# Last modulation beside w_o, seven products from the second FFN slab on, and another order of pairs in the last projection

## The chip, the cores and the metric

The kernel runs on one core of a Trainium2 chip. The metric is the device time of one execution in microseconds; the time before is the median of three runs. All times in the text are microseconds.

## The reference

One layer of a decoder trunk on x of 256 rows (SEQ) by 2048 columns (D), with a condition c; all in f32.

```python
# each layer
mod = SiLU(c) @ ada_w + ada_b -> (shift1, scale1, gate1, shift2, scale2, gate2)
h   = RMSNorm(x) * (1 + scale1) + shift1
h @ w_in + b_in  -> RG-LRU input, GeLU gate, q, k, v, branch gates
branch A: conv -> RG-LRU * GeLU(gate) -> w_lru
branch B: sliding-window attention -> w_att
merged = sigmoid(g_A) * A + sigmoid(g_B) * B
x  += gate1 * (merged @ w_o)
h2  = RMSNorm(x) * (1 + scale2) + shift2
x  += gate2 * SwiGLU(h2)          # hidden width 5632
out = RMSNorm(x)
```

## The kernel before

**Products.** Every f32 weight block is split into a high part `hi` (f32r, cast by ACT, L305) and a rest `lo` (`raw - hi`, DVE, L317), and so is every activation. A product is then three matmuls in `mm3`: L355 (hi by hi), L356 (lo of one side), L357 (lo of the other). A matmul has 512 columns in all the places that matter here.

**Items.** The program is a list of items, each one load of 512 KB (128 x 1024 f32, `raw`, L288, on SP's queue) and twelve matmuls as a rule. `step(i)` emits one item after the other: it issues the load of item i + 5, makes hi up to item i + 3 and lo up to item i + 2, then the matmuls. `raw` has five buffers, `hi` four, `lo` three. Since each engine and each DMA queue works in the order of emission, this sets what stands behind what. SP's queue holds nearly all DMAs.

**Work on the side.** Beside the items, generators (`Side`) emit attention, scan and modulations in small steps. A planner (`run_sides`) emits a step when its own estimate of the busy times of PE, DVE, ACT and DMA has room before the end of the present item, and when the condition that the step yields is true. It charges 1.46 per load of 512 KB, and nothing for the loads of xr, g1 and x1d.

**Modulations.** The first five are made by `ada_cols` (L496: multiply and reduce, 158 halves `aw` of 512 KB). The sixth, gate2, is made by `ada_rows` (the side `ada_ffn`): 32 loads `aw` of 512 KB (L467), a memset of `pa` on POOL (L677), a load of the bias row into `pa` (L678, SP), 32 DVE rows that accumulate `aw * c` into `pa` (L685), and four small products with a row of ones that spread the sum over the partitions (L691, L693). It starts when the condition of its first `yield` is true. The buffer of `pa` is shared with the row of c that `ada_cols` uses.

**Stages, by item number of before.** 244 to 275: w_o, four slabs of eight items. At its start `w_o_first` loads x again as `xr0` to `xr3` (L1034) and sends gate1 through memory: `g1_row` is copied by ACT (L1013), written as `g1d` (L1015) and read back broadcast as `g10`, `g11` (L1018). Each w_o slab ends with `yo = wo * g1` (L1055; L1100 in the last) and `xr += yo` (L1057, L1101), and the result is kept in `x1d` (L1041). After w_o comes the second norm (L1100 to L1141), and then eleven FFN slabs: `fg` and `fu`, whose result `ft` is transposed by PE (L954). Slabs below `SLAB_7` are plain (`add_slab`, 192 matmuls). From `SLAB_7` on `add_pair` computes three of the eight 2 x 2 quads of blocks (k = 4, 8, 12) by Winograd's form with seven products instead of eight (`seven`), whose sums of weights, `made`, are emitted by DVE (L418 to L425) into buffers that `ada_rows` uses as well; `all_modulations` therefore finishes `ada_ffn` ahead of slab `SLAB_7`.

**Last projection.** It has two sweeps over pairs k = 0, 2, 4, ... of hidden blocks: n = 0 (`w_f2a`) and n = 2 (`w_f2d`). The pairs in `SEVEN` (6, 10, ..., 34) are Winograd quads (`seven_last`: sums `last`, `ah`, `al`), the others plain. The pairs from `EARLY` (36) on are plain and, in the second sweep, follow as items of other matrices. After the last quad `combined(n)` (L1390 to L1399) adds the shared products, and `blocks` (L1415, L1417, L1441) adds the residual and norm weight to finished blocks. The blocks of the first sweep are finished beside the start of the second one. The program ends with the late products, the last norm (L1469 to L1515) and the stores.

Of the kernel before, what the change touches and what calls it, by code (L numbers as in the profile page):

```python
# [21 lines left out]
NH = HID // P  # L22
# [40 lines left out]
N_MADE, N_HOLD = 5, 4  # L63
SEVEN = tuple(range(6, 36, 4))

SEVEN_1, SLAB_7 = (4, 8, 12), 3
EARLY = NH - 2 * N_HOLD

N_SPARE = 5
# [5 lines left out]
def hybrid_layer(  # L75
# [19 lines left out]
    def free(b4=0, m=0):  # L95
        used["b4"] -= b4
        used["m"] -= m
# [11 lines left out]
    def mtile(name):  # L109
        used["m"] += 1  # L110
        return sum_bank(name)
# [372 lines left out]
    def ada_cols(todo, halves):  # L484

        yield 0, 0
        for group in todo:
            for j in range(2):
                for m, kt in group:
                    v = V_ADA + m * NK + kt  # L490
                    dst = modc[:, m, kt:kt + 1]
                    if not halves.got:
                        halves.fetch()
                    yield CH * T_DVE + 0.1, 0, 0, 0, halves.here
                    r = halves.take()
                    nc.vector.tensor_tensor_reduce(  # L496
                        out=r, in0=r, in1=crow[:, j * CH:(j + 1) * CH], op0=ALU.mult, op1=ALU.add, scale=1.0,
                        scalar=dst if j else vec[:, v:v + 1], accum_out=dst,
                    )
                    halves.fetch()  # L500
            for m, kt in group:
                if m in (1, 4):
                    g, dst = (V_N1 if m == 1 else V_N2) + kt, modc[:, m, kt:kt + 1]
                    nc.vector.scalar_tensor_tensor(dst, dst, 1.0, vec[:, g:g + 1], op0=ALU.add, op1=ALU.mult)
                cols_done.add((m, kt))
# [162 lines left out]
    def ada_rows():  # L668

        got = Halves([ada_g[kt, :, j * CH:(j + 1) * CH] for kt in range(NK) for j in range(2)])  # L670
        got.spare = lambda: len(got.got) - got.own < N_SPARE
        yield 0, 0, 0, 0, lambda: bool(h2)
        streams.append(got)
        got.fetch()

        pa = ap_.tile([P, D], F32, tag="pal", name="pa")
        nc.gpsimd.memset(pa, 0.0)  # L677
        nc.sync.dma_start(pa[0:1, :], bg_row)  # L678
        for kt in range(NK):
            for j in range(2):  # L680
                if not got.got:
                    got.fetch()
                yield CH * T_DVE, 0, 0, 0, got.here
                p = pa[:, j * CH:(j + 1) * CH]
                nc.vector.scalar_tensor_tensor(p, got.take(), cact[:, kt:kt + 1], p, op0=ALU.mult, op1=ALU.add)  # L685
                got.fetch()
        for c in range(4):
            yield 0, 0, 0, 1
            pb = mtile(f"pb{c}")
            cs = slice(c * 512, (c + 1) * 512)  # L690
            nc.tensor.matmul(pb, lhsT=ones, rhs=pa[:, cs], start=True, stop=True)  # L691
            yield 0, 0.55
            nc.scalar.copy(pa[:, cs], pb)  # L693
            free(m=1)
        bcs[5] = pa
# [393 lines left out]
    h2, h_sum = {}, {}  # L1089
# [241 lines left out]
    def out_products(jobs, t2=(0, 1), hold=None, after=None):  # L1331

        def go(hi, lo):
            if hold is not None:
                hold.extend((hi, lo, j) for j in jobs)
            if jobs[0][:2] == (0, 0):
                last_first()
                sides.append(Side(fetch_last()))
            for t in t2:
                for kt in sorted({j[0] for j in jobs}):  # L1340
                    ah, al = fact(kt)
                    mine = [j for j in jobs if j[0] == kt]
                    for k, (l, w) in enumerate(((ah, hi), (ah, lo), (al, hi))):
                        for _, n, c0 in mine:
                            nc.tensor.matmul(  # L1345
                                bank(t, n), lhsT=l[:, rows(t)], rhs=w[:, c0:c0 + 512], start=kt == 0 and k == 0,
                                stop=kt == (EARLY - 2 if (t, n) == (1, 3) else NH) - 1 and k == 2, skip_group_check=True,
                            )
            if after is not None:
                after()  # L1350
        return go

    def seven_last(k, n, src):
        parts = {}

        def parts_high():
            hi = parts[0] = wp.tile([P, 8, P], F32R, tag="araw", name=f"ah{n}_{k}", bufs=N_ADA)
            nc.scalar.copy(hi[:, 0:7, :], f_sum[k][:, 0:7, :])
            return 0, 0.9

        def parts_low():
            lo = parts[1] = b4(f"al{n}_{k}", F32R, (8, P))
            nc.vector.tensor_tensor(lo[:, 0:7, :], f_sum[k][:, 0:7, :], f32(parts[0][:, 0:7, :]), op=ALU.subtract)
            return 1.0, 0

        def own(to):
            if to not in "pqru":
                return bank(int(to[0]), n + int(to[1]))
            if k == SEVEN[0]:
                fin[to] = sum_bank(f"p{to}{n}")  # L1370
            return fin[to]

        items[-3].before.append(parts_high)
        items[-2].before.append(parts_low)
        seven(
            (src[k], src[k + 1]), {(0, 0): (0, 0), (0, 1): (0, 512), (1, 0): (1, 0), (1, 1): (1, 512)},
            lambda a: [parts[h][:, a, :] for h in range(2)], own, k == SEVEN[0], k == SEVEN[-1],
            lambda i: fin["made"][:, i * CH:(i + 1) * CH], (lambda: combined(n)) if k == SEVEN[-1] else None,
        )
# [46 lines left out]
    def blocks(n0, n1):  # L1426

        def post():
            last = None
            for n in range(n0, n1):  # L1430
                for t in range(2):
                    g = residual(t, n)
                    next(g)
                    if last is not None:
                        next(last, None)
                    last = g
                    yield 1.2, 0.7
            next(last, None)
            for t in range(2):
                x2 = fin["x2"][:, t, n0 * 512:n1 * 512]  # L1440
                nc.vector.tensor_tensor(x2, x2, fin["fg"][:, n0 * 512:n1 * 512], op=ALU.mult)  # L1441
                yield 0.6 * (n1 - n0), 0.7 * (1 - t)
        return post

    for n, src in ((0, w_f2a), (2, w_f2d)):
        for k in range(0, NH if n == 0 else EARLY, 2):
            if k in SEVEN:
                seven_last(k, n, src)
                continue
            for kt in (k, k + 1):  # L1450
                items.append(Item(
                    src[kt], CH, out_products([(kt, n, 0), (kt, n + 1, 512)]), blocks(0, 2) if kt == NH - 1 else None,
                ))
# [74 lines left out]
    todo = iter([(decay, 0)] + [(f, g) for f in (lru, attention) for g in range(4)])  # L1528
    mix = [Side(mixers(todo)) for _ in range(2)]
    ada_ffn = Side(ada_rows())  # L1530

    cols = [[(m, kt) for m in (1, 0) if m == 0 or kt >= N_K] for kt in range(NK)]
# [4 lines left out]
    ada = Side(ada_cols(cols, halves), 3)  # L1537
# [151 lines left out]
```

## Time and profile before

| what | us |
|---|---|
| median of three runs | 1553.1 |
| range of the three | 1551.76 to 1557.28 |
| the profiled execution, its own time | 1555.14 |
| its span in the trace | 1553.4 |
| PE busy | 1534.8 (99%) |
| DVE busy | 1359.0 (87%) |
| ACT busy | 843.8 (54%) |
| mean granted clock of PE | 0.997 |
| w_o on PE | 743.4 to 831.9 |
| the 32 rows of `pa` (L685) | 860.8 to 955.1 |

PE is the matmul engine, PEld its weight load, which overlaps it. DVE makes all `lo` parts and adds, ACT the `hi` parts, POOL does almost nothing, and SP issues the DMAs. In a timeline a row has start, duration, engine, line, operation, output and inputs, the number of instructions drawn together, and in brackets the idle time before and what ended it. A matmul's duration there (0.39) is that of a pipelined instruction; the distance of two starts is what it costs. The rows of the windows view give stretch and length, then the busy time of PE, weight load, DVE, ACT and POOL with numbers of instructions, the granted clock, the share of the DMA engines and GB/s.

### The profile page before, as it was taken

How to read it: one execution, taken by the hardware profiler on the slowest of the kernel's cores; microseconds unless marked ns; L12 is line 12 of the kernel's file. 1: busy time of each engine (PE TensorE's matmuls, PEld its weight loads, DVE VectorE, ACT ScalarE, POOL GpSimd, SP SyncE). 2: the span in 40 equal slices, each digit the busy share in tenths (PEclk: the TensorE clock that was granted, in tenths of full speed). 3: DMA queues.
4: the chain of work that ended last, by engine and by line, in shares of the span. 5: the costliest groups of instructions: out<-in, count | busy, mean ns of one | idle time of the engine just before them, and what ended most of it. 6: DMA issues, size and time to landing. Idle time of an engine off the chain costs nothing.

```text
span 1553.4 us, 22040 instructions
## 1 busy us (share of the span) xinstructions
PE 1534.8 (99%) x8031; PEld 1318.1 (85%) x8031; DVE 1359.0 (87%) x1804; ACT 843.8 (54%) x1083; POOL 3.9 (0%) x9
## 2 busy tenths in 40 slices
PE   9999999999999999999999999999999999999997
PEld 7999999998878887888888888888888888888886
DVE  7889989899888887989657997899999998998998
ACT  4654443776855445444445544555555555665664
POOL 0000000000000000000000000000000000000000
PEclk9999999999999999999999999999999999999999
DMA  9999998665787797999867998555656665766563
GB/s 367 342 322 343 338 314 297 205 217 190 271 283 251 263 332 269 369 340 334 270 218 232 347 341 273 176 192 201 203 191 198 207 193 202 284 205 210 193 209 116
DMA packets 112910, 400.38 MB, mean 258 GB/s; under 512 B 12433, under 2 KB 12577, under 8 KB 112417
## 3 DMA queue, kind: packets, MB, share of 16 engines
q1 hardware_dynamic: 112514, 398.46, 74.6%
q8 instruction: 63, 1.03, 0.3%
q10 hardware_dynamic: 288, 0.52, 0.1%
q14 instruction: 45, 0.37, 0.1%
HBM read 394.73 MB, written 4.20 MB: 257 GB/s over the span
## 4 chain that ended last, share of the span: by engine, by line
PE 94%; DMA 3%; DVE 2%; issue 0%; ACT 0%; SPq 0%; DVEq 0%; ACTq 0%
PE pf L1345 9%; PE wi L357 6%; PE wi L356 6%; PE wi L355 6%; PE f L357 6%; PE f L356 6%; PE f L355 6%; PE wga L356 2%; PE wga L357 2%; PE wga L355 2%; PE wo L355 2%; PE wo L356 2%; PE wa L356 2%; PE wa L355 2%; PE wa L357 2%; PE wo L357 2%
## 5 line engine op out<-in xcount | busy, mean ns | idle before, releaser
L305 ACT CAST hi<-raw 128x1024 fp32r<-128x1024 f32 (+1 forms) x540 | 540.5, 1008 | 487.8 <-PE wi L356 78.7
L317 DVE TENSOR_TENSOR lo<-raw,hi 128x1024 fp32r<-128x1024 f32 (+1 forms) x540 | 622.6, 1165 | 114.2 <-issue 45.0
L357 PE MATMUL wi<-h_both,lo 128*128 128x256 f32 x800 | 227.4, 284 | 3.4 <-DVE lo L317 3.4
L355 PE MATMUL wi<-h_both,hi 128*128 128x256 f32 x800 | 228.0, 285 | 0.0
L356 PE MATMUL wi<-h_both,hi 128*128 128x256 f32 x800 | 227.1, 284 | 0.0
L357 PEld LDWEIGHTS wi<-h_both,lo 128*128 128x128 f32 x800 | 154.3, 193 | 3.9 <-DVE lo L317 3.8
L355 PEld LDWEIGHTS wi<-h_both,hi 128*128 128x128 f32 x800 | 154.2, 193 | 0.3
L356 PEld LDWEIGHTS wi<-h_both,hi 128*128 128x128 f32 x800 | 154.2, 193 | 0.2
L355 PE MATMUL f<-hi,h_both 128*128 128x512 f32 x368 | 144.3, 392 | 0.0
L357 PE MATMUL f<-hi,h_both 128*128 128x512 f32 x368 | 143.2, 389 | 0.0
L356 PE MATMUL f<-lo,h_both 128*128 128x512 f32 x368 | 143.2, 389 | 0.0
L496 DVE CUSTOM_DVE_ANT_0 aw<-aw,crow,vec 128x1024 f32<-128x1024 f32 x79 | 100.6, 1278 | 6.5 <-DMA aw<-in_ada_t_dram 6.5
L496 DVE CUSTOM_DVE_ANT_0 aw<-aw,crow,modc 128x1024 f32<-128x1024 f32 x79 | 100.8, 1279 | 5.7 <-DMA aw<-in_ada_t_dram 5.7
L305 ACT CAST hi<-made 128x1024 fp32r<-128x1024 f32 x48 | 50.7, 1057 | 90.7 <-PE f L357 86.4
L357 PEld LDWEIGHTS f<-hi,h_both 128*128 128x128 f32 x368 | 69.1, 188 | 14.4
L356 PEld LDWEIGHTS f<-lo,h_both 128*128 128x128 f32 x368 | 69.1, 188 | 14.3 <-issue 0.2
L355 PEld LDWEIGHTS f<-hi,h_both 128*128 128x128 f32 x368 | 69.1, 188 | 14.3 <-ACT hi L305 0.2
L317 DVE TENSOR_TENSOR lo<-made,hi 128x1024 fp32r<-128x1024 f32 x48 | 58.8, 1225 | 20.5 <-PE f L356 17.3
L1345 PE MATMUL pf<-hi,fc 128*128 128x512 f32 x256 | 71.0, 389 | 0.0
L305 ACT CAST hi<-last 128x1024 fp32r<-128x1024 f32 x32 | 33.8, 1055 | 53.9 <-PE pf L1345 52.2
L1345 PEld LDWEIGHTS pf<-hi,fc 128*128 128x128 f32 x256 | 48.0, 188 | 9.9
L355 PE MATMUL wl<-hi,yh 128*128 128x512 f32 x128 | 52.5, 410 | 0.0
(353 smaller groups left out, 3078.7 us busy)
## 6 DMA issues: line engine op xcount, KB each, us to landing
raw<-in_w_f_dram SPq DMA_DIRECT2D x176, 512.0 KB, 4.4
raw<-in_w_in_dram SPq DMA_DIRECT2D x164, 512.0 KB, 6.8
aw<-in_ada_t_dram SPq DMA_DIRECT2D x158, 512.0 KB, 6.4
raw<-in_w_f2a_dram SPq DMA_DIRECT2D x44, 512.0 KB, 4.4
raw<-in_w_f2d_dram SPq DMA_DIRECT2D x36, 512.0 KB, 4.3
raw<-in_w_lru_dram SPq DMA_DIRECT2D x32, 512.0 KB, 6.6
raw<-in_w_att_dram SPq DMA_DIRECT2D x32, 512.0 KB, 8.4
raw<-in_w_o_dram SPq DMA_DIRECT2D x32, 512.0 KB, 4.6
```

The costliest lines, as they stand in the source:

```text
L305: nc.scalar.copy(hi[:, cs], live[i][0][:, cs])
L317: nc.vector.tensor_tensor(lo[:, cs], raw[:, cs], f32(hi[:, cs]), op=ALU.subtract)
L355: nc.tensor.matmul(ps, lhsT=lh, rhs=rh, start=start, stop=False, skip_group_check=True)
L356: nc.tensor.matmul(ps, lhsT=lh, rhs=rl, start=False, stop=False, skip_group_check=True)
L357: nc.tensor.matmul(ps, lhsT=ll, rhs=rh, start=False, stop=stop, skip_group_check=True)
L496: nc.vector.tensor_tensor_reduce(out=r, in0=r, in1=crow[:, j * CH:(j + 1) * CH], op0=ALU.mult, op1=ALU.add, scale=1.0, scalar=dst if j els ...
L1345: nc.tensor.matmul(bank(t, n), lhsT=l[:, rows(t)], rhs=w[:, c0:c0 + 512], start=kt == 0 and k == 0, stop=kt == (EARLY - 2 if (t, n) == (1, ...
```

## The change

Three edits. The condition on which `ada_rows` starts becomes "the other modulations are done" instead of "the second norm has been emitted". `SLAB_7` goes from 3 to 1, so that slabs 1 and 2 become `add_pair`. In each sweep of the last projection the pairs below `EARLY` are taken in another order: before 0, 2, 4, 6s, 8, 10s, ..., 32, 34s, and now 0, 2, 6s, 4, 10s, 8, ..., 34s, 32, where s marks a quad of seven products.

```diff
-SEVEN_1, SLAB_7 = (4, 8, 12), 3
+SEVEN_1, SLAB_7 = (4, 8, 12), 1
...
-        yield 0, 0, 0, 0, lambda: bool(h2)
+        yield 0, 0, 0, 0, lambda: ada.cost is None
         streams.append(got)
         got.fetch()
...
     for n, src in ((0, w_f2a), (2, w_f2d)):
-        for k in range(0, NH if n == 0 else EARLY, 2):
+
+        others = [k for k in range(0, EARLY, 2) if k not in SEVEN]
+        turns = others[:2] + [k for two in zip(SEVEN, others[2:]) for k in two]
+        for k in turns + list(range(EARLY, NH if n == 0 else EARLY, 2)):
             if k in SEVEN:
                 seven_last(k, n, src)
                 continue
```

Lines behind the third edit have a number that is higher by 3 in the changed kernel. PE has 18 matmuls fewer. Of the 32 rows of `pa`, 27 now stand in w_o and five in FFN slab 0.

**Start of w_o, SP.** In these rows `raw` is a weight item, `aw` a half of a modulation's weights, and `pa` the bias row. Before, behind the last half of the fifth modulation:

```order
L467 DMA aw157_7253<-in_ada_t_dram 128x1024
L288 DMA raw245_7272<-in_w_o_dram 128x1024
L288 DMA raw246_7293<-in_w_o_dram 128x1024
L288 DMA raw247_7312<-in_w_o_dram 128x1024
L288 DMA raw248_7330<-in_w_o_dram 128x1024
```

Now:

```order
L467 DMA aw157_7253<-in_ada_t_dram 128x1024
L288 DMA raw245_7272<-in_w_o_dram 128x1024
L288 DMA raw246_7293<-in_w_o_dram 128x1024
L467 DMA aw0_7312<-in_ada_g_dram 128x1024
L678 DMA pa_7314<-in_bg_row_dram 1x2048
L288 DMA raw247_7317<-in_w_o_dram 128x1024
L467 DMA aw1_7323<-in_ada_g_dram 128x1024
```

The load of the bias row, which waits for POOL's memset of `pa`, stands ahead of raw247.

**Middle of the first w_o slab, SP.** Before, with `xr` the rows of x and `g1d`, `g10`, `g11` the way of gate1 through memory:

```order
L288 DMA raw251_7389<-in_w_o_dram 128x1024
L288 DMA raw252_7417<-in_w_o_dram 128x1024
L1034 DMA xr0_7423<-in_x_r_dram 128x2x512
L1034 DMA xr1_7425<-in_x_r_dram 128x2x512
L1034 DMA xr2_7427<-in_x_r_dram 128x2x512
L1034 DMA xr3_7429<-in_x_r_dram 128x2x512
L1015 DMA g1d_171<-g1_row_7433 16x128
L1018 DMA g10_7436<-g1d_171 128x1024
L1018 DMA g11_7438<-g1d_171 128x1024
L288 DMA raw253_7456<-in_w_o_dram 128x1024
L288 DMA raw254_7476<-in_w_o_dram 128x1024
```

Now:

```order
L467 DMA aw4_7409<-in_ada_g_dram 128x1024
L288 DMA raw252_7434<-in_w_o_dram 128x1024
L467 DMA aw5_7440<-in_ada_g_dram 128x1024
L1034 DMA xr0_7442<-in_x_r_dram 128x2x512
L1034 DMA xr1_7444<-in_x_r_dram 128x2x512
L1034 DMA xr2_7446<-in_x_r_dram 128x2x512
L1034 DMA xr3_7448<-in_x_r_dram 128x2x512
L1015 DMA g1d_171<-g1_row_7452 16x128
L1018 DMA g10_7455<-g1d_171 128x1024
L1018 DMA g11_7457<-g1d_171 128x1024
L288 DMA raw253_7475<-in_w_o_dram 128x1024
L467 DMA aw6_7481<-in_ada_g_dram 128x1024
```

Five halves (aw1 to aw5) have moved ahead of `g1d`, the last two of them shown here, and aw6 stands behind raw253.

**The same place, DVE.** `lo253` is what PE's item 253 needs; `yo0` closes the first w_o slab. Before:

```order
L317 TENSOR_TENSOR lo251_7480<-raw251_7389,hi251_7458 128x1024
L317 TENSOR_TENSOR lo252_7498<-raw252_7417,hi252_7478 128x1024
L317 TENSOR_TENSOR lo253_7516<-raw253_7456,hi253_7496 128x1024
L1055 TENSOR_TENSOR yo0_7530<-wo0_0_0_7356,g10_7436 128x512
L1055 TENSOR_TENSOR yo0_7530<-wo0_0_1_7357,g10_7436 128x512
L317 TENSOR_TENSOR lo254_7537<-raw254_7476,hi254_7514 128x1024
```

Now:

```order
L317 TENSOR_TENSOR lo251_7502<-raw251_7403,hi251_7477 128x1024
L685 SCALAR_TENSOR_TENSOR pa_7314<-aw5_7440,cact_110,pa_7314 128x1024
L317 TENSOR_TENSOR lo252_7523<-raw252_7434,hi252_7500 128x1024
L685 SCALAR_TENSOR_TENSOR pa_7314<-aw6_7481,cact_110,pa_7314 128x1024
L317 TENSOR_TENSOR lo253_7542<-raw253_7475,hi253_7521 128x1024
L685 SCALAR_TENSOR_TENSOR pa_7314<-aw7_7504,cact_110,pa_7314 128x1024
L1055 TENSOR_TENSOR yo0_7559<-wo0_0_0_7368,g10_7455 128x512
L1055 TENSOR_TENSOR yo0_7559<-wo0_0_1_7369,g10_7455 128x512
L317 TENSOR_TENSOR lo254_7566<-raw254_7498,hi254_7540 128x1024
```

A row of `pa` stands ahead of lo252, lo253 and `yo0`, each with its own load to wait for.

**Start of the second sweep, DVE.** `y` and the `last` behind it (L1415, L1417, L1441) are blocks of the first sweep, L418 to L425 the sums of weights of the sweep's first seven products, and the two `lo` from `last` are what these read. Before (items 566 to 569 are the seven products):

```order
L317 TENSOR_TENSOR lo565_13104<-raw565_13032,hi565_13082 128x1024
L1441 TENSOR_TENSOR last_12091<-last_12091 128x1024
L418 TENSOR_TENSOR last_12091<-raw566_13058 128x512
L419 TENSOR_TENSOR last_12091<-raw566_13058,raw567_13080 128x512
L317 TENSOR_TENSOR lo566_13126<-raw566_13058,hi566_13102 128x512
L1363 TENSOR_TENSOR al2_6_13128<-fs1_8905,ah2_6_13106 128x896
L1441 TENSOR_TENSOR last_12091<-last_12091 128x1024
L424 TENSOR_TENSOR last_12091<-raw567_13080,last_12091 128x512
L425 TENSOR_TENSOR last_12091<-raw567_13080,last_12091 128x512
L317 TENSOR_TENSOR lo567_13149<-raw567_13080,hi567_13124 128x1024
L317 TENSOR_TENSOR lo568_13167<-last_12091,hi568_13147 128x1024
L317 TENSOR_TENSOR lo569_13177<-last_12091,hi569_13165 128x1024
```

Now (items 576 to 579):

```order
L419 TENSOR_TENSOR last_12183<-raw576_13103,raw577_13124 128x512
L317 TENSOR_TENSOR lo576_13176<-raw576_13103,hi576_13150 128x512
L1363 TENSOR_TENSOR al2_6_13178<-fs1_8982,ah2_6_13154 128x896
L1415 TENSOR_TENSOR y1_512_13192<-pf11_12195,pa_7314 128x512
L1417 TENSOR_TENSOR last_12183<-y1_512_13192,last_12183 128x512
L424 TENSOR_TENSOR last_12183<-raw577_13124,last_12183 128x512
L425 TENSOR_TENSOR last_12183<-raw577_13124,last_12183 128x512
L317 TENSOR_TENSOR lo577_13202<-raw577_13124,hi577_13174 128x1024
L1441 TENSOR_TENSOR last_12183<-last_12183 128x1024
L317 TENSOR_TENSOR lo578_13222<-last_12183,hi578_13200 128x1024
L1441 TENSOR_TENSOR last_12183<-last_12183 128x1024
L317 TENSOR_TENSOR lo579_13233<-last_12183,hi579_13220 128x1024
```

The seven products' rows now stand among the block rows of the first sweep, two plain `lo` earlier.

## The prediction

> **What bounds the kernel now.** I read the page first (busy shares, slices, chain), then the busy time by stretch, then the timelines of the engines at the four places that the change touches.
>
> ```profile
> PE 1534.8 (99%) x8031; PEld 1318.1 (85%) x8031; DVE 1359.0 (87%) x1804; ACT 843.8 (54%) x1083; POOL 3.9 (0%) x9
> PE 94%; DMA 3%; DVE 2%; issue 0%; ACT 0%; SPq 0%; DVEq 0%; ACTq 0%
> ```
>
> PE works 99% of the span and is 94% of the chain. A removed matmul is therefore worth its step, and every idle PE microsecond is added to the time. DVE at 87% is the engine that can become late.
>
> ```profile
> 50.00:52.00 2.00, 1.90 (x14) 1.54 (x12) 0.05 (x1) 1.68 (x3) 0.00 (x0) 1.00 1.04 414
> ...
> 740.00:760.00 20.00, 20.00 (x94) 16.62 (x94) 12.11 (x12) 8.54 (x10) 0.66 (x1) 1.00 0.74 231
> 760.00:780.00 20.00, 20.00 (x90) 16.57 (x89) 10.64 (x10) 8.61 (x11) 0.00 (x0) 1.00 0.92 332
> 860.00:900.00 40.00, 40.00 (x183) 33.19 (x182) 37.53 (x46) 21.28 (x28) 0.00 (x0) 1.00 0.97 359
> 1021.80:1064.10 42.30, 42.30 (x193) 35.10 (x192) 39.29 (x49) 23.90 (x28) 0.00 (x0) 1.00 0.60 199
> ```
>
> Each row: stretch, its length, busy time of PE, weight load, DVE, ACT and POOL, granted clock, DMA share, GB/s. The first, from the start of the kernel, shows the highest rate that I need: 414 GB/s. The next two are the w_o stretch: DVE has 8 to 9 us of 20 free, but the DMA engines are already 0.92 busy at 760 to 780. At 860 to 900, FFN slab 0 with the modulation beside it, DVE is nearly full and DMA at 0.97 with 359 GB/s. The last is a slab with seven products: DVE 39.3 of 42.3, so it fits.
>
> **Seven products in slabs 1 and 2.** The transposes after each slab mark the pitch, and three matmuls in a row the step.
>
> ```profile
> 886.85 1.03 PE L954 MATMUL ft<-ident,sg 128*128 128x128 f32 x8
> 931.26 1.03 PE L954 MATMUL ft<-ident,sg 128*128 128x128 f32 x8
> 979.23 1.03 PE L954 MATMUL ft<-ident,sg 128*128 128x128 f32 x8
> 1021.61 1.03 PE L954 MATMUL ft<-ident,v 128*128 128x128 f32 x8
> ...
> 1444.23 0.39 PE L355 MATMUL pp<-hi,ah 128*128 128x512 f32 x1
> 1444.45 0.39 PE L356 MATMUL pp<-lo,ah 128*128 128x512 f32 x1
> 1444.68 0.39 PE L357 MATMUL pp<-hi,al 128*128 128x512 f32 x1
> ```
>
> A plain slab takes 44.41 us (931.26 less 886.85), one with seven 42.38 (1021.61 less 979.23): 2.03 us. That is nine matmuls at the step of some 0.226 us (three products of a Winograd step fewer, each of three f32r matmuls). Two slabs: **-4.1 us**, with ends of -3.9 and -4.2. The extra DVE work (24 sums, 12 more lo, 14 rows that join the products) is what the last stretch above shows as fitting. Slab 1 no longer has `pa` rows beside it, slab 0 only five of them, so DVE stands better there than at 860 to 900.
>
> **The last modulation beside w_o.** It adds no work: 32 loads of 512 KB, a memset, a small row load and 32 DVE rows move from slabs 0 to 2, 27 of them into w_o. What the move passes is SP's queue, where the weights, xr and g1 are issued in order.
>
> ```profile
> 729.36 10.92 SPq L288 DMA_DIRECT2D raw<-in_w_o_dram  x5
> 748.37 2.02 SPq L1034 DMA_DIRECT2D xr<-in_x_r_dram  x4
> 753.29 0.35 SPq L1015 DMA_DIRECT2D g1d<-g_row  x1
> 758.07 0.83 SPq L1018 DMA_DIRECT2D g<-g1d  x2
> 758.99 8.94 SPq L288 DMA_DIRECT2D raw<-in_w_o_dram  x6
> ...
> 738.84 1.81 POOL L677 MEMSET pa<- 128x2048 f32 x1 [513.10 <-DVE modc L496]
> ...
> 765.27 1.05 ACT L305 CAST hi<-raw 128x1024 fp32r<-128x1024 f32 x1 [5.73 <-PE wo L357]
> ...
> 761.04 1.23 DVE L317 TENSOR_TENSOR lo<-raw,hi 128x1024 fp32r<-128x1024 f32 x1 [1.49 <-PE wo L356]
> 766.35 1.23 DVE L317 TENSOR_TENSOR lo<-raw,hi 128x1024 fp32r<-128x1024 f32 x1 [4.09 <-ACT hi L305]
> 767.50 1.28 DVE L1055 TENSOR_TENSOR yo<-wo,g 128x512 f32<-128x512 f32 x2
> ...
> 769.39 0.39 PE L356 MATMUL wo<-lo,mh 128*128 128x512 f32 x1
> ...
> L685 DVE SCALAR_TENSOR_TENSOR pa<-aw,cact,pa 128x1024 f32<-128x1024 f32 x32 | 40.9, 1278 | 0.0
> ```
>
> This is the tightest place of w_o already. SP sends g1 through memory: g1d out at 753.29, back only after it landed (758.07), and raw253 stands behind both, issued at 758.99. Its hi began at 765.27, 6.3 us after issue; its lo ended at 767.5 (the next DVE row starts there); PE read it at 769.39. The margin is 1.9 us.
>
> After the change SP first stops at the load of bg_row, which waits for the memset of `pa`: that ends at 738.84 + 1.81 = 740.65. Raw247, the third of the five loads in the first row before, goes out at 741. Then 15 loads of 512 KB stand ahead of g1d (raw247 to 252, aw1 to aw5, xr0 to xr3), where there were ten, over a longer time. Each takes 1.27 us at the fullest rate the trace shows (414 GB/s), 1.46 us at 359; I take 1.30. With some 3 us from issue to the first bytes: 744 + 15 x 1.30 = 763.5 for g1d instead of 758.07, 5.4 us later. raw253 is then issued at 764.4 and its hi starts 6.3 us later, at 770.7, ending at 771.8. On DVE pa6 stands ahead of its lo, and aw6 is issued behind raw253: 1.30 later, 772.0, then 1.20 for pa6 and 1.15 for lo: 774.4. PE wants it at 769.39: **idle of 5.0 us**. Bounds: no latency and the fastest rate gives g1d at 741 + 15 x 1.27 = 760.1 and 1.6 us of idle; 359 GB/s gives 765.9 and 7.6 us.
>
> What an idle PE does to its clock is seen once:
>
> ```profile
> 52.00:54.00 2.00, 0.07 (x1) 0.07 (x1) 1.69 (x3) 2.00 (x6) 0.00 (x0) 1.00 1.01 395
> 54.00:56.00 2.00, 2.00 (x13) 2.00 (x14) 2.00 (x2) 2.00 (x4) 0.00 (x0) 0.75 0.96 332
> 56.00:58.00 2.00, 2.00 (x12) 2.00 (x11) 2.00 (x3) 2.00 (x6) 0.00 (x0) 0.50 1.06 351
> 58.00:60.00 2.00, 2.00 (x17) 2.00 (x17) 2.00 (x4) 1.23 (x3) 0.00 (x0) 0.90 0.95 353
> ```
>
> Two microseconds of idle, then 0.75, 0.50 and 0.90 of the clock: 2 x (0.25 + 0.50 + 0.10) = 1.7 us lost. An idle of 5 us pays that too (0 if it is split into short ones). The term is **+6.7 us**, from 1.6 to 9.3. The Trainium skill (TensorE: Matmul & The Clock Gate, Part 1) puts the fall to half clock after an idle window of about 3.4 us; by that rule an estimate of the price of a 5 us idle is the same 1.7 us, and an idle of 2 us would be free, which the rows at 52 to 58 contradict. The sum needs only the rows.
>
> Later in w_o each item brings 1.95 loads of all kinds (raw, 0.8 aw, a share of x1d write-back): 2.54 us at 1.30, below its 2.72 us of PE (12 steps), and DVE needs 1.13 + 1.20 = 2.33 (a lo, a `pa` row). So no further stall, but little is regained: the cover is thin.
>
> **Second norm.** The chain to FFN's first matmul starts with yo3:
>
> ```profile
> 829.04 1.23 DVE L317 TENSOR_TENSOR lo<-raw,hi 128x1024 fp32r<-128x1024 f32 x1 [1.49 <-PE wo L356]
> 830.57 0.69 DVE L1100 TENSOR_TENSOR yo<-wo,g 128x512 f32<-128x512 f32 x1 [0.30 <-PE wo L357]
> ```
>
> Now pa26 (1.20 us) stands between the two, in a gap of 0.30: **+0.9 us** (0, if it ran earlier, to 1.3). The four small products of `pa` move from the first third of slab 2 to the end of slab 0 at the same price: nothing.
>
> **Order of the last sweeps.** Start of the second sweep first:
>
> ```profile
> 1426.52 0.69 DVE L1415 TENSOR_TENSOR y<-pf,pa 128x512 f32<-128x512 f32 x1 [0.31 <-PE pf L1345]
> ...
> 1444.56 2.35 DVE L317 TENSOR_TENSOR lo<-last,hi 128x1024 fp32r<-128x1024 f32 x2
> ```
>
> From 1426.52 DVE works off the finished blocks without a pause worth naming (0.34 us in all) and ends the second lo of the first seven at 1446.8. The first seven now begins one pair (24 matmuls, 5.44 us) earlier, at 1438.8 on the clock of before, and wants this lo 16 steps later, at 1442.4. DVE loses two plain lo (1.13 each) and the pauses ahead of it: 1446.8 - 2.27 - 0.34 = 1444.2. PE idles **1.8 us** (0 if other DVE rows fall behind, to 2.5). In the first sweep no blocks are pending and I see no stall.
>
> The end:
>
> ```profile
> 1516.96 1.23 DVE L317 TENSOR_TENSOR lo<-last,hi 128x1024 fp32r<-128x1024 f32 x1 [0.29 <-ACT hi L305]
> ...
> 1544.96 0.42 DVE L1415 TENSOR_TENSOR y<-late,pa 128x256 f32<-128x256 f32 x1
> ...
> 1542.34 0.28 PE L357 MATMUL late<-hi,fl 128*128 128x256 f32 x1
> ```
>
> PE ends at 1542.62, the DVE row on its last product starts at 1544.96: DVE is 2.3 us behind, from work that begins with the last seven. That now comes 5.44 us earlier with two more lo (2.27) before the end: 3.2 us less, of which only the 2.3 can be used. **-2.2 us** (0 to -2.3).
>
> **Sum**, against the profiled execution (span 1553.4, run 1555.14): -4.1 + 6.7 + 0.9 + 1.8 - 2.2 = **+3.1 us**. That run lies 2.0 us above the median of the three runs; the difference is put on the median: 1553.1 + 3.1 = 1556.2.
>
> **Rivals.**
> 1. SP's detour is hidden: g1d lands by about 759.5, so that lo253 is still in time. For it: DMA runs at only 0.74 at 740 to 760, aw0 is issued before the stop. Against: fifteen loads after 741 need 19 us. The place is item 253, the point of decision 1.9 us. Then -4.1 - 2.2 + 0.9 + 1.8 = -3.6, or 1549.5; without the two small stalls 1546.8. This ends on the faster side.
> 2. The transfers bind the whole of w_o: at 359 GB/s (1.46 us a load) an item's 1.95 loads take 2.85 us of 2.72, 0.13 x 22 = 2.9 us more, and the first stall is 7.6 + 1.7: 1553.1 + 3.1 + 2.6 + 2.9 = 1561.7. For it: 0.97 share at 359. Against: 414 at 50 us. The Trainium skill (DMA: Bandwidth & Descriptors, Specifications) states about 358 GB/s of HBM per core, which is this rival; the 414 GB/s row speaks against it.
> 3. The seven products bring nothing since DVE is late in slab 1: without the -4.1 it is 1560.3. Against: 39.3 of 42.3 in the slabs that have them.
>
> **Chances.** Forecast 0.62 (own range 1552 to 1560), hidden 0.23, transfers bind 0.10, nothing from seven 0.05. The range leaves out the fastest part of the first rival and most of the second: 1548 to 1560.5. A measurement tells about 0.5%, 7.8 us: below 1545.3 counts as faster, above 1560.9 as slower. The terms that gain add up to 6.3 us, so faster needs more than the change offers (0.04); slower is rival 2 and a part of 3 (0.11).
>
> **What would show it.** w_o: SP idle until 740.7, g1d issued or landed near 763, one PE gap of about 5 us at item 253 with a clock below 1 behind it. Slabs 1 and 2: transposes 42.4 us apart. Second norm: pa ahead of yo3. Second sweep: a PE gap of 1 to 2 us in its first seven. End: the last product's DVE row directly behind PE's end. Wrong: no gap in w_o, or many small ones.

## The result, and the profile after

The changed kernel takes 1564.9 us (median of six runs, 1562.3 to 1570.2) against 1552.8 before (six runs as well; 1553.1 was the median of the first three): a ratio of 1.0078, 95% interval 1.0055 to 1.0100. It is slower, by 12 us or 0.8%; the forecast was 3 us, and the range ended at 1560.5. Its profiled execution took 1562.41 us, with a span of 1560.6. The page's first and fourth parts, of after:

```profile
PE 1534.3 (98%) x8013; PEld 1316.3 (84%) x8013; DVE 1392.5 (89%) x1854; ACT 853.5 (55%) x1097; POOL 3.8 (0%) x9
PE 91%; DMA 5%; DVE 2%; issue 1%; SPq 0%; ACT 0%; DVEq 0%; ACTq 0%
```

PE's share of the chain fell from 94 to 91%, and DMA has taken most of what PE lost (3 to 5%).

Stage by stage, the difference is read from the first and last L355 matmul of a tile (columns: count; shortest, median and longest duration in ns; first and last start). `fg` belongs to the FFN, `pp` is the first product of each quad of seven in the last projection, and `late` are the products at its end. The row for w_o, of after:

```profile
L355 PE MATMUL wo<-hi,mh x128: 389/389/796, 742.2 to 840.6; 128*128 128x512 f32 x128
```

All stretches read in this way, with a second profile of the changed kernel (the run "again" below):

| stretch, us | before | after | again |
|---|---|---|---|
| start to the first matmul of w_o | 743.7 | 742.2 | 743.8 |
| w_o, first to last L355 | 87.3 | 98.4 | 97.6 |
| second norm, to the first of `fg` | 6.2 | 8.1 | 12.6 |
| FFN, to the first `pp` | 492.8 | 483.2 | 484.3 |
| first to last `pp` of the two sweeps | 185.6 | 187.6 | 187.6 |
| last `pp` to the last `late` | 26.5 | 32.0 | 31.9 |
| to the end of the span | 11.3 | 9.1 | 9.2 |

The pair that moved behind the last quad takes 5.5 us out of the fourth row and puts them into the sixth. So the parts of the change measure: w_o +11.1 and +10.3, second norm +1.9 and +6.4, slabs 1 and 2 -4.1 (9.6 less 5.5; -3.1 in the second profile, where a slow clock reached into the FFN), second sweep +2.0, end -2.2. The first row is no effect that can be read: in the thirteen profiles of this text, w_o began anywhere between 740.1 and 745.2.

The gap in w_o, PE's timeline of after (in brackets the idle time and what ended it):

```profile
767.45 0.39 PE L357 MATMUL wo<-hi,ml 128*128 128x512 f32 x1
772.78 0.80 PE L355 MATMUL wo<-hi,mh 128*128 128x512 f32 x1 [4.94 <-ACT hi L305]
776.20 0.79 PE L356 MATMUL wo<-lo,mh 128*128 128x512 f32 x1 [2.62 <-DVE lo L317]
776.79 0.63 PE L357 MATMUL wo<-hi,ml 128*128 128x512 f32 x1
777.22 0.63 PE L355 MATMUL wo<-hi,mh 128*128 128x512 f32 x1
...
781.84 0.40 PE L357 MATMUL wo<-hi,ml 128*128 128x512 f32 x1
```

It is the item that the prediction named, with hi and then lo missing: 7.6 us of idle. Behind it the step is 0.43 us instead of 0.23, half clock, until 781.5: the 13 steps from 776.20 to 781.84 take 5.6 us instead of 2.9. With the 0.8 us of the lone matmul between the two waits this is the +11.1. What held it, from SP, ACT and DVE of after:

```profile
739.19 0.30 SPq L678 DMA_DIRECT2D pa<-in_bg_row_dram  x1
...
753.49 0.33 SPq L467 DMA_DIRECT2D aw<-in_ada_g_dram  x1
753.87 2.66 SPq L1034 DMA_DIRECT2D xr<-in_x_r_dram  x4
756.63 0.48 SPq L1015 DMA_DIRECT2D g1d<-g_row  x1
764.85 0.81 SPq L1018 DMA_DIRECT2D g<-g1d  x2
765.72 0.42 SPq L288 DMA_DIRECT2D raw<-in_w_o_dram  x1
...
771.68 1.04 ACT L305 CAST hi<-raw 128x1024 fp32r<-128x1024 f32 x1 [13.63 <-DMA raw<-in_w_o_dram]
...
773.72 1.28 DVE L685 SCALAR_TENSOR_TENSOR pa<-aw,cact,pa 128x1024 f32<-128x1024 f32 x1 [12.13 <-DMA aw<-in_ada_g_dram]
774.92 1.22 DVE L317 TENSOR_TENSOR lo<-raw,hi 128x1024 fp32r<-128x1024 f32 x1
```

SP stops for the memset, then until 753.49, when aw5 goes out as a row of `pa` ends on DVE, then for g1d's 8 KB: 8.2 us from issue to the next issue, where it was 4.8 before. Now aw5 and the four xr have only just been issued ahead of it; before, the xr had gone out from 748.37 on, 4.9 us ahead of g1d. Counted from the first matmul of w_o, g1d goes out 4.8 us later than before and is back 8.3 us later. raw253 goes out at 765.72, and the `pa` row ahead of its lo waits two us longer than the hi.

The windows of the same stretch, of after:

```profile
742.00:762.00 20.00, 20.00 (x94) 16.64 (x93) 17.89 (x18) 7.32 (x9) 0.00 (x0) 1.00 0.99 361
744.00:764.00 20.00, 20.00 (x94) 16.66 (x93) 15.89 (x15) 6.79 (x9) 0.00 (x0) 1.00 0.94 346
764.00:766.00 2.00, 2.00 (x10) 1.65 (x10) 0.00 (x0) 0.00 (x0) 0.00 (x0) 1.00 0.10 22
764.00:784.00 20.00, 12.44 (x41) 9.33 (x41) 10.11 (x10) 6.46 (x9) 0.00 (x0) 0.74 0.92 334
784.00:832.00 48.00, 48.00 (x214) 39.75 (x213) 43.10 (x39) 22.84 (x28) 0.00 (x0) 1.00 1.01 369
```

And two of before, the start of the program and the stretch of the last row:

```profile
10.00:50.00 40.00, 37.59 (x263) 35.45 (x262) 32.71 (x60) 19.06 (x42) 0.00 (x0) 1.00 1.03 403
784.00:832.00 48.00, 48.00 (x215) 39.72 (x214) 26.92 (x27) 21.94 (x28) 0.00 (x0) 1.00 0.63 199
```

From 742 to 762, while the loads ahead of g1d pass, the DMA engines are full, share 0.99, and carry 361 GB/s: 1.45 us for 512 KB. Behind the gap, for 48 us, it is 369 GB/s or 1.42 us. That is the price that a load has here, not 1.30. At the start of the program full engines carry 403 GB/s for 40 us, which is 1.30 us; why they carry less in w_o, no run shows. From 764 to 766 they stand nearly still (0.10): SP waits for g1d and has issued nothing behind it.

### The profile page after: what moved, and what is told of

The parts are those of the page before. It is cut to its first block, busy times and chain, and to the rows that moved or that the text cites. A ratio compares the mean times of both kernels' runs of the same rounds, so it can differ in the third digit from the quotient of the medians.

```text
span 1560.6 us, 22091 instructions
## 1 busy us (share of the span) xinstructions
PE 1534.3 (98%) x8013; PEld 1316.3 (84%) x8013; DVE 1392.5 (89%) x1854; ACT 853.5 (55%) x1097; POOL 3.8 (0%) x9
## 4 chain that ended last, share of the span: by engine, by line
PE 91%; DMA 5%; DVE 2%; issue 1%; SPq 0%; ACT 0%; DVEq 0%; ACTq 0%
PE pf L1345 9%; PE f L357 7%; PE f L356 7%; PE f L355 7%; PE wi L357 6%; PE wi L356 6%; PE wi L355 6%; PE wga L357 2%; PE wga L355 2%; PE wga L356 2%; PE wa L357 2%; PE wa L356 2%; PE wa L355 2%; PE wl L356 2%; PE wl L357 2%; PE wl L355 2%
## 5 line engine op out<-in xcount | busy, mean ns | idle before, releaser
L355 PE MATMUL wi<-h_both,hi 128*128 128x256 f32 x800 | 228.0, 285 | 0.0
L355 PE MATMUL f<-hi,h_both 128*128 128x512 f32 x460 | 180.2, 392 | 0.0
L357 PE MATMUL f<-hi,h_both 128*128 128x512 f32 x460 | 179.0, 389 | 0.0
L356 PE MATMUL f<-lo,h_both 128*128 128x512 f32 x460 | 179.0, 389 | 0.0
L355 PEld LDWEIGHTS wi<-h_both,hi 128*128 128x128 f32 x800 | 154.3, 193 | 0.2
L305 ACT CAST hi<-made 128x1024 fp32r<-128x1024 f32 x60 | 63.4, 1056 | 112.8 <-PE f L357 111.0
L357 PEld LDWEIGHTS f<-hi,h_both 128*128 128x128 f32 x460 | 86.3, 188 | 17.9
L356 PEld LDWEIGHTS f<-lo,h_both 128*128 128x128 f32 x460 | 86.4, 188 | 17.8 <-issue 0.2
L355 PEld LDWEIGHTS f<-hi,h_both 128*128 128x128 f32 x460 | 86.4, 188 | 17.8 <-issue 0.2
L317 DVE TENSOR_TENSOR lo<-made,hi 128x1024 fp32r<-128x1024 f32 x60 | 73.4, 1225 | 25.7 <-PE f L356 20.4
L685 DVE SCALAR_TENSOR_TENSOR pa<-aw,cact,pa 128x1024 f32<-128x1024 f32 x32 | 41.0, 1282 | 20.8 <-DMA aw<-in_ada_g_dram 20.2
```

The lines of the kernel that those rows point to most:

```text
L305: nc.scalar.copy(hi[:, cs], live[i][0][:, cs])
L317: nc.vector.tensor_tensor(lo[:, cs], raw[:, cs], f32(hi[:, cs]), op=ALU.subtract)
L355: nc.tensor.matmul(ps, lhsT=lh, rhs=rh, start=start, stop=False, skip_group_check=True)
L356: nc.tensor.matmul(ps, lhsT=lh, rhs=rl, start=False, stop=False, skip_group_check=True)
L357: nc.tensor.matmul(ps, lhsT=ll, rhs=rh, start=False, stop=stop, skip_group_check=True)
```

## Experiments

Ratios are to the kernel before on the same chip, with 95% intervals.

**again**: the changed kernel unaltered, for a second profile.

> The changed kernel once more, for a second profile on the chip of the runs below. Theory (queue): the same one gap at item 253, about 5 us without hi and 2.6 us without lo, then half clock for some 6 us; w_o takes 104 to 109 us from its first matmul to the first of the FFN against 93.5 before. If the spread of the six runs (1562 to 1570) is the clock behind the gap, the mean clock falls with the time (0.995 at 1562, 0.992 at 1570). Rival (bandwidth): the gaps wander over w_o from run to run.

1566.3 us, 1.0070 (1.0053 to 1.0087). The gap stood at item 253 again, 4.0 us without hi and 2.5 without lo, and w_o lost nearly the same (10.3). From the first matmul of w_o to the first of the FFN it took 110.2 us, a little above the expected 104 to 109. What differs between the two profiles is the second norm, which the expectation had not named. Timelines of PE and DVE, and the granted clock, of again:

```profile
847.80 0.33 PE L1080 MATMUL pt<-ident,xr 128*128 128x128 f32 x1 [2.89 <-DVE xr L1101]
...
841.87 1.28 DVE L685 SCALAR_TENSOR_TENSOR pa<-aw,cact,pa 128x1024 f32<-128x1024 f32 x1 [0.72 <-DMA aw<-in_ada_g_dram]
843.07 1.22 DVE L317 TENSOR_TENSOR lo<-raw,hi 128x1024 fp32r<-128x1024 f32 x1
845.13 1.28 DVE L685 SCALAR_TENSOR_TENSOR pa<-aw,cact,pa 128x1024 f32<-128x1024 f32 x1 [0.84 <-DMA aw<-in_ada_g_dram]
846.34 0.68 DVE L1100 TENSOR_TENSOR yo<-wo,g 128x512 f32<-128x512 f32 x1
...
850.00:852.00 2.00, 1.45 (x5) 1.02 (x4) 0.48 (x3) 0.70 (x2) 0.00 (x0) 0.50 1.00 316
852.00:854.00 2.00, 2.00 (x11) 1.94 (x10) 1.46 (x4) 1.13 (x3) 0.00 (x0) 0.50 1.01 297
854.00:856.00 2.00, 2.00 (x7) 1.61 (x7) 1.82 (x5) 0.94 (x3) 0.00 (x0) 0.50 0.99 285
```

Each `pa` row waits for its load, everything behind it on DVE is late, `yo3` starts 4 us after the last product, and this second gap drops the clock once more. In the first profile the loads came a little earlier (`yo3` 0.7 us behind), and the clock held.

**hold**: no load of the modulation ahead of g1.

```diff
-        yield 0, 0, 0, 0, lambda: ada.cost is None
+        yield 0, 0, 0, 0, lambda: ada.cost is None and len(g1) == 2
```

> The last modulation may start only when g10 and g11 are in SP's queue, so its loads all stand behind g1d and the bias row is no longer ahead of raw247. Theory (queue): PE's gap at item 253 falls from 8.3 us to under 2, the clock stays at 1 there, and the time is 1552.8 - 4.1 - 2.2 + 2.0 (second sweep) + 2.0 (second norm) + 0 to 2 = 1550.5 to 1552.5. Rival (bandwidth: w_o has more bytes than the DMA engines carry in its time): the gap only moves, 5 us or more somewhere later in w_o, 1558 or more.

1566.0 us, 1.0074 (1.0053 to 1.0096). The order does decide the one large gap: w_o took 92.1 us, with four gaps of 0.3 to 1.3 us and the clock at 1. But nothing was gained. The second norm took 8.9, and the rows that no longer fit into w_o and slab 0 were forced in one block ahead of slab 1:

```profile
889.68 3.67 DVE L685 SCALAR_TENSOR_TENSOR pa<-aw,cact,pa 128x1024 f32<-128x1024 f32 x3
892.25 6.10 PE L691 MATMUL pb<-pa,ones 128*128 128x512 f32 x8 [5.15 <-issue]
```

FFN to the first `pp` took 491.1 instead of 483.2: PE waited 5.15 us for the block, and the granted clock was 0.50 from 892 to 896. Neither theory was right alone.

**nostop**: no memset and no bias load ahead of raw247.

```diff
-        nc.gpsimd.memset(pa, 0.0)
-        nc.sync.dma_start(pa[0:1, :], bg_row)
...
+                if kt == 0:
+                    nc.vector.tensor_scalar(p, got.take(), cact[:, kt:kt + 1], None, op0=ALU.mult)
...
+            nc.sync.dma_start(br[0:1, :], bg_row[:, cs])
+            nc.vector.tensor_tensor(pa[0:1, cs], pa[0:1, cs], br[0:1, :], op=ALU.add)
```

> The first rows of pa write instead of accumulating, so that the memset is gone, and the bias row is loaded and added at the end of the modulation: SP no longer stops for POOL ahead of raw247. Number and order of the large loads stay. Theory (the stop is a good part of it): g1d is issued some 4 us earlier (752 instead of 756), PE's gap at item 253 is about 4 us instead of 8.3, time about 1558 to 1560. Rival (the count of loads and the wait of aw5 for its DVE row set it): gap of 7 to 8 us, 1562 to 1570 as the changed kernel.

1568.7 us, 1.0087 (1.0070 to 1.0103). g1d went out 3 us earlier, counted from the first matmul of w_o, and the gap was 2.0 + 2.6 us: that half of the expectation held, w_o 95.2. The time did not follow, since the second norm took 12.1 and PE waited 2.5 us for the added bias rows ahead of `pb`. Only the gap can be read from this run.

**pool**: the way of g1 through memory on POOL's queue.

```diff
-        nc.sync.dma_start(g1d, row[0:NK, 0:P])
+        nc.gpsimd.dma_start(g1d, row[0:NK, 0:P])
...
-            nc.sync.dma_start(
+            nc.gpsimd.dma_start(
                 g1[i], g1d[8 * i:8 * i + 8, :].rearrange("k p -> (k p)").partition_broadcast(P)
```

> g1d, g10 and g11 are issued from POOL's queue instead of SP's; all else as in the changed kernel, the 15 loads ahead included. Theory (SP standing still for g1d's round trip): raw253 is issued at about 757 instead of 765.7, its hi starts near 763, no gap at item 253 or one below 1 us, 1550 to 1553. Rival (bandwidth): raw253 is issued early but lands after 768 since the DMA engines are full, gap of 3 us or more, 1556 or more.

1562.5 us, 1.0047 (1.0032 to 1.0062). SP issued raw253 at 755.34, 8.7 us earlier than in the changed kernel, counted from the first matmul of w_o, yet:

```profile
764.79 1.05 ACT L305 CAST hi<-raw 128x1024 fp32r<-128x1024 f32 x1 [8.28 <-DMA raw<-in_w_o_dram]
...
767.34 1.28 DVE L685 SCALAR_TENSOR_TENSOR pa<-aw,cact,pa 128x1024 f32<-128x1024 f32 x1 [6.80 <-DMA aw<-in_ada_g_dram]
...
769.82 0.80 PE L356 MATMUL wo<-lo,mh 128*128 128x512 f32 x1 [3.42 <-DVE lo L317]
```

The load took 9.4 us to its hi, and the next one, aw6, held DVE for 6.8. The wait for hi is gone, the one for lo stayed: the rival, a full DMA, took over. w_o 94.1, second norm 11.9.

**slim**: the same loads, 64 KB each; seven eighths of the modulation's weights are left out.

```diff
+                if self.slim:
+                    nc.sync.dma_start(t[:, 0:128], self.srcs[self.n][:, 0:128])
+                else:
+                    nc.sync.dma_start(t, self.srcs[self.n])
...
+                few = got.take()[:, 0:128].unsqueeze(1).broadcast_to([P, 8, 128])
+                nc.vector.scalar_tensor_tensor(p8, few, cact[:, kt:kt + 1], p8, op0=ALU.mult, op1=ALU.add)
```

> The loads of the last modulation carry 128 of their 1024 columns (64 KB instead of 512 KB), and the DVE row reads these eight times over, so its length stays; number, order and waits of the instructions stay as in the changed kernel. The modulation's values are wrong by this. Theory (bytes: the DMA engines are full from 744 on, a load costs 1.42 to 1.46): w_o takes 88 to 89 us again instead of 98, second norm at most 1 us longer than before, clock 1 throughout, time 1552.8 - 4.1 - 2.2 + 2.0 + 0.9 = about 1549 to 1551. Rival (queue: SP's stop at the bias row and aw5's wait for its DVE row hold g1d back whatever the bytes): g1d is issued near 756 again, a gap of 3 us or more at item 253 stays, 1554 or more.

1555.8 us against 1554.0, 1.0009 (1.0000 to 1.0019). Without the bytes w_o took 91.8 and the second norm 6.9. The windows of slim:

```profile
764.00:784.00 20.00, 17.70 (x71) 13.91 (x70) 16.95 (x16) 9.36 (x12) 0.00 (x0) 0.91 0.92 311
784.00:832.00 48.00, 48.00 (x213) 39.77 (x212) 43.35 (x39) 23.14 (x29) 0.00 (x0) 1.00 0.74 244
```

Some six of the eleven us in w_o, and all but 0.7 of the second norm, went with the bytes. (The profiled execution was the fastest of ten, 1553.5, so this share is rather too large than too small.) A gap of 1.25 + 1.05 us, with a clock of 0.91 over these 20 us, stayed at item 253: less than the 3 us of the rival, but the time is in its range. Without the bytes SP still reached aw5 only 9.3 us behind the first matmul of w_o (11.3 in the changed kernel), and g1d took 7.0 us to the next issue.

**slimpool**: slim and pool together.

> The 64 KB loads of the run slim, and g1d, g10, g11 on POOL's queue: both causes away, each alone left a gap at item 253 (2.3 us and 3.4 us). Again the modulation's values are wrong by the short loads. Theory (bytes and the round trip of g1 on SP's queue together make the gap, nothing else does): no gap at item 253, w_o 87.5 us from first to last L355 as before, second norm 0.5 to 1 us longer; 1554 - 4.1 - 2.2 + 2.0 + 0.7 = about 1550.5, 2 to 5 below slim. Rival (the DVE rows of pa ahead of lo are a third cause): a gap of 1 us or more stays, 1553 or more.

1550.9 us against 1553.7, 0.9983 (0.9974 to 0.9992). No gap at item 253, w_o 87.7, second norm 6.9, clock 1:

```profile
764.00:784.00 20.00, 20.00 (x89) 16.25 (x88) 19.45 (x18) 9.67 (x13) 0.00 (x0) 1.00 0.89 299
784.00:832.00 48.00, 48.00 (x222) 39.97 (x221) 43.83 (x41) 22.49 (x29) 0.00 (x0) 1.00 0.69 233
```

DVE does all the rows of `pa` there (19.5 of 20 us busy) and PE does not wait for it, though SP's stop at the bias row stayed (739.02). This closes the account of w_o: the bytes and g1's round trip on SP's queue make the gap together, each alone leaves one, and DVE's own time makes none.

**norm**: no row of `pa` from the lo of item 274 on until the second norm is emitted.

```diff
-                yield CH * T_DVE, 0, 0, 0, got.here
+                yield CH * T_DVE, 0, 0, 0, lambda: got.here() and (at["lo"] < 274 or bool(h2))
```

> The changed kernel, but no row of pa is emitted once the lo of item 273 stands, until the second norm has been emitted; the rows left over go to FFN slab 0. Theory (pa rows that wait for late loads delay the norm's chain): from the last matmul of w_o to the first of the FFN 5.7 us as before instead of 7.7 and 12.6 (two profiles of the changed kernel), clock 1 there, the gap at item 253 unchanged; 1564.9 to 1566.3 less 2 to 7 = 1559 to 1563, and a smaller spread. Rival: the rows moved to slab 0 are forced in one block ahead of slab 1 (as with the start held back) and PE waits there for 2 to 5 us: no gain.

1568.7 us, 1.0095 (1.0080 to 1.0110). The second norm took 6.5 us, so the `pa` rows ahead of `yo3` are its delay. The rival won on the time: PE waited 4.0 us for the forced block ahead of slab 1, and the FFN took 490.0.

**order**: the order of pairs alone (third edit).

> The order of pairs in the last sweeps alone, all else as before. Theory: +2.0 at the first seven of the second sweep, -2.2 behind PE's end: 1552 to 1554, no difference that can be measured. Rival: the sweep's start is only late because of the clock and the lateness of the changed kernel: then -2.2, 1550.5.

1552.6 us against 1554.0, 0.9997 (0.9986 to 1.0009). The two sweeps took 187.6 between first and last `pp` (+2.0), the end 9.0 (-2.3). They cancel.

**part1**: the early start alone (first edit).

> The early start of the last modulation alone (SLAB_7 = 3 and the old order). Theory (all of the loss is in w_o and the second norm, the other two parts are worth -4.1 and -0.2): 1565 + 4.3 = 1569, between 1566 and 1573. Rival (seven products in slabs 1 and 2 add to the loss): at or below 1565.

1567.8 us, 1.0095 (1.0079 to 1.0111). w_o 97.6, second norm 12.0, the rest as before. The whole loss is in this edit.

**late2** and **late3**: versions meant to beat both, with the order of before. The diff is late2; late3 has 264 for 258 and 272 for 274.

```diff
-SEVEN_1, SLAB_7 = (4, 8, 12), 3
+SEVEN_1, SLAB_7 = (4, 8, 12), 2
...
-        yield 0, 0, 0, 0, lambda: bool(h2)
+        yield 0, 0, 0, 0, lambda: ada.cost is None and len(g1) == 2 and at["load"] >= 258
...
+                yield CH * T_DVE, 0, 0, 0, lambda: got.here() and (at["lo"] < 274 or bool(h2))
```

> A version meant to beat both, with the order of pairs of before: the last modulation starts in w_o, but only behind g1 and from the load of item 258 on, no row of pa stands beside the second norm, and seven products begin with slab 2 (one slab gained, 2.0 us). Theory (w_o bears some 14 of the 32 loads if none stands ahead of g1, since the DMA engines have 30% of their time free there): 1554 - 2.0 = about 1552, no gap in w_o. Rival (bandwidth binds for the 40 us in which each item brings its own load and one more): gaps of 1 to 3 us in w_o, 1553 to 1556.

1553.2 us against 1553.7, 0.9994 (0.9986 to 1.0003). w_o 87.4, second norm 6.1, FFN 490.7 against 492.8: the trace has the 2.0 us of one slab and no gap, although the DMA engines are full from 764 to 832. So full engines alone cost nothing here; in the changed kernel the loads that filled them stood ahead of g1d, and so ahead of raw253.

```profile
764.00:784.00 20.00, 20.00 (x90) 16.57 (x89) 15.08 (x14) 9.67 (x12) 0.00 (x0) 1.00 1.02 392
784.00:832.00 48.00, 48.00 (x213) 39.74 (x213) 38.60 (x35) 22.97 (x28) 0.00 (x0) 1.00 1.01 373
```

A gain of 0.06% is within what the runs can tell from none: it beats the changed kernel, and the kernel before not clearly.

> As late2, but starting from the load of item 264, with eight rows of pa in w_o and three of them in one block at the end of slab 1. Theory: no gap in w_o, PE waits up to 3 us for that block ahead of slab 2; 1552 to 1555. Rival (slab 1 has room): 1552, as late2.

1558.8 us, 1.0035 (1.0022 to 1.0048). PE waited 4.4 us for the block ahead of slab 2, and its mean clock was 0.92 over 45 us. The rival "slab 1 has room" fell, and the time lies above the 1555 of the theory too.

## Why the prediction was wrong

**Seven products in slabs 1 and 2: right.** -4.1 predicted and measured. The transposes of after:

```profile
901.86 1.04 PE L954 MATMUL ft<-ident,sg 128*128 128x128 f32 x8
944.24 1.03 PE L954 MATMUL ft<-ident,v 128*128 128x128 f32 x8
986.61 1.03 PE L954 MATMUL ft<-ident,v 128*128 128x128 f32 x8
```

Slab 1 and slab 2 take 42.38 and 42.37. One reading beside it was wrong, without a consequence: the small products of `pa` ran at 959.3 to 973.3 of before, in the second half of slab 2 and not in its first third.

**The order of the sweeps: right.** +1.8 predicted, +2.0 measured; -2.2 predicted and measured. PE in the first seven of the second sweep, and DVE at the end, of after:

```profile
1449.29 0.50 PE L356 MATMUL pr<-lo,ah 128*128 128x512 f32 x1 [0.61 <-DVE lo L317]
1451.56 0.50 PE L356 MATMUL pq<-lo,ah 128*128 128x512 f32 x1 [0.62 <-DVE lo L317]
...
1552.01 0.42 DVE L1415 TENSOR_TENSOR y<-late,pa 128x256 f32<-128x256 f32 x1 [0.50 <-PE late L357]
```

PE's two waits add up to 1.2 of the 2.0 us; the matmul behind each is longer (0.50). At the end, the last DVE row now waits for PE, as the bound of the term said.

**The gap in w_o: right in place and mechanism, short in size.** +6.7 predicted, +10.3 to +11.1 measured, above the upper bound of 9.3. The step that failed is "I take 1.30" for a load. The row of 860 to 900 (0.97, 359 GB/s, 1.46 us), where the same loads of the modulation run, was at hand, and I set the 414 GB/s of 50 to 52 against it. The 414 was no short peak: full engines carry 403 GB/s from 10 to 50, and two-us windows of before reach 420 in w_o itself (768 to 770). But over longer stretches of w_o full engines carried less: 361 from 742 to 762 in the changed kernel, and 356 to 377 (1.39 to 1.47 us) from 784 to 832 in the eight runs whose share is 0.99 to 1.01 there. Put into the prediction's own sum, raw247 at 739.59, 3 us of latency and g1d back at 764.85 make 1.48 us for each of the 15 loads. By 1.46 that sum gave 7.6 us of idle; measured are 7.6, or 8.3 with the one matmul that PE did in between. The sum counts no wait of SP for the buffers of `aw`; in the changed kernel the full engines covered it (0.99 from 742 to 762), while in slim, without the bytes, it showed. The clock was the second error: two gaps 3.4 us apart cost one fall, but a longer one, 2.7 us instead of 1.7.

The Trainium skill (DMA: Bandwidth & Descriptors, Where 436 GB/s comes from) names about 358 GB/s of HBM per core as the limit that binds between HBM and SBUF. The windows of w_o are near it, those from 10 to 50 (403 GB/s) are above it; no run shows that it is what binds in w_o. The rival with 1.46 us a load (1561.7) came nearest, in part by luck: it held 2.9 us of later waits in w_o that did not come, and no more for the second norm than the forecast.

**The second norm: wrong.** +0.9 predicted, up to 1.3, as the length of one DVE row. Measured are +1.9, +6.4 and, in part1, +5.8. The step "pa26 (1.20 us) stands between the two" counted the row and not its wait. With full DMA engines the loads of the last rows come late, so that DVE comes late to `yo3`; in again, the chain of the norm then left PE idle long enough for the clock to fall again. Without the bytes it was +0.7, without these rows +0.3 (norm). This term is also most of what differs between the changed kernel's two profiles.

**"So no further stall, but little is regained".** In w_o that held: behind item 253 PE waited 0.2 us at most. The lateness went on in DVE to the end of w_o, where the second norm paid.

**The sum.** 3.1 predicted. By profiles: +11.1, +1.9, -4.1, +2.0, -2.2 and -1.5 ahead of w_o make the 7.2 between the spans; the column of again adds up to 13.6 in the same way. The 12 us between the medians lie between 7.2 and 13.6: the profiled execution of before was 2.3 us above its median, that of after 2.5 below.

## What to carry to other kernels

Work moved into a stretch where one engine has room must be priced on all the queues that it crosses: at the start of w_o DVE had 40% free, and DMA, at 0.92 in its worst 20 us, had not. Take the price of a load from full engines near the place, with the same transfers: in this program full engines carried 403 GB/s in one long stretch and some 360 in another. A row that waits for a transfer costs its engine the wait, and every instruction behind it too; keep such rows out of the last steps ahead of a serial chain, but leave them a place before the next deadline, or the forced block costs as much.

## What the runs showed that was not expected

The clock fell without a single long gap. In slim PE had two gaps, 1.25 and 1.05 us, within four us, and the granted clock was 0.50 at 770 to 772; in hold a lone gap of 1.34 us, followed by three in the next 22 us, left it at 1.00.

```profile
766.00:768.00 2.00, 0.75 (x5) 0.29 (x3) 0.95 (x1) 1.04 (x1) 0.00 (x0) 1.00 0.96 357
768.00:770.00 2.00, 0.95 (x3) 0.59 (x4) 2.00 (x3) 1.04 (x1) 0.00 (x0) 0.99 0.97 381
770.00:772.00 2.00, 2.00 (x7) 1.51 (x6) 2.00 (x4) 1.04 (x1) 0.00 (x0) 0.50 1.00 389
```

PE was busy for 1.7 of the four us ahead of the fall. The Trainium skill (TensorE: Matmul & The Clock Gate, Part 1) gives an idle window of about 3.4 us as the condition; the rows of slim fit a low share of busy time in a window of that kind better than idle alone. Where PE was busy for a little more, the clock stayed at 1.00: 2.15 of the four us from 838 to 842 in hold, and 2.3 from 844 to 848 in the changed kernel. No run separates the two.

An 8 KB transfer is as late as what is ahead of it: g1d took 8.2 us to the next issue right behind 2.5 MB, and 4.8 before, when the 2 MB ahead of it had a start of 4.9 us. On POOL's queue the same transfer still held POOL for 6.0 us, but SP no longer stood still for it.
